# A hybrid decoder layer on one core: 64 more tokens take their first expert product from gathered rows, and the blocks are staged anew

## The chip, the core and the metric

The kernel runs on one core of one Trainium2 chip. A core has five engines that run their own instruction queues in order: TensorE (PE, with its weight loads shown apart as PEld), VectorE (DVE), ScalarE (ACT), GpSimd (POOL) and SyncE (SP), which here only issues DMAs. The metric is the device time of one execution in microseconds (us); lower is better.

## The reference, cut to what matters

One layer on 512 tokens of width 1024: normalisation, three kinds of attention, an output projection, and then a feed-forward part (PEER) that picks experts. All that changes lies in PEER:

```
qry = (h @ w_q) ...                       # 8 heads
s1, s2 = qry halves @ sub1, sub2          # 128 scores each
top 16 of each, top 16 of their sums  ->  expert (8 x 16 = 128 slots per token), gate = softmax
a   = einsum('cd,ced->ce', x, u[expert])  # first product: 16384 experts, rows of 1024
w   = gelu(a) * gate
out = einsum('ce,ced->cd', w, v[expert])  # second product
```

## The kernel before, in words

Tokens are cut into four chunks of 128. **Chunk 0** is done as the reference says: for each of its 128 slots an indirect DMA on POOL gathers one row of `u` per token (`gather`, four row buffers), and one DVE instruction multiplies it with the token's vector and sums it up (line 481, "dot" below). After a gelu the same is done with rows of `v` (line 488).

**Chunks 1 to 3** (384 tokens) are done densely: the 16384 experts are 128 blocks of 128. For a block `a_block` computes the product of the block of `u` with all 384 tokens, in split precision: both sides are cut into a high and a low part (`split`, lines 85 and 86: ACT makes the high part, DVE the low one), and `mm3` does three matmuls for each of eight slices of the width, so 24 matmuls of 384 columns. ACT takes the gelu out of PSUM, where two banks ("t") hold such products. `w_block` multiplies it with the gates of this block (`gt`, zero where a token did not pick the expert), splits the product and the block of `v`, and adds 18 matmuls of 512 columns to the output.

The gates come from a table `gd` in DRAM (12 pieces of 32 tokens). It is written in the **scatter stage**: for each four tokens DVE makes one-hot rows (line 586, then four times line 590), PE multiplies them (line 593) and ACT copies the result (line 594). There are 96 such groups of four. No `w_block` can run before all of the table is written.

So blocks of `u` come in two kinds. **Early blocks** (`NSP`, 64) only need `a_block`, and run beside routing and scatter; their gelus go to DRAM (`ad`) and come back later, but for the last `KEEP` = 16, which stay in SBUF ("kept"). The room of the kept tiles is that of the scatter stage's tiles, so the kept blocks run after it. The other blocks run together with the `w_block`s of all 128 in the **last stage**. After each early block one step of chunk 0's gathers follows in the program text.

The order on each engine is not that of the program text: it is set when the kernel is built, by a scheduler which estimates when each instruction can start. Each engine then runs its list in order.

Of the kernel before, what the change touches and what calls it, by code (L numbers as in the profile page):

```python
# [22 lines left out]
P = 128  # L23
# [14 lines left out]
NSP = 64  # L38
# [9 lines left out]
KEEP = 16  # L48
TD = P * len(DC)
# [6 lines left out]
def layer_kernel(ctx, tc, x, xT, memT, mem, w_in, w_kv, w_out, w_q, cols, qk_gain, g_bc, subT, bias_tab,  # L56
# [11 lines left out]
    gd = dram.tile([TD // GT, P, NK, GT], F32, name="gd")  # L68
# [285 lines left out]
    def mix_out(chunks, yT, rg, hT, name):  # L354
        n_c = len(chunks)
        with tile_pool(name=f"wo{name}", bufs=2) as wo:
# [55 lines left out]
    def route(c, dst=None, q0=0, nq=PH):  # L412
# [95 lines left out]

    def u_parts(b, i, e_lo):
        ur = flat().rearrange("p (k e) -> p k e", e=NK)  # L510
        DMA.dma_start(ur, uT[b])
        halves[b] = [t.rearrange("p k t -> p (k t)")[:, i * D:(i + 1) * D].rearrange("p (k e) -> p k e", e=NK)
                     for t in yT]
        last_lo.append(split(*halves[b], ur, e_lo))

    def a_block(b):
        us = halves.pop(b)
        ap = bank("t")[:, :TD]
        for k in range(KD):
            mm3(ap, [t[:, k, :] for t in us], [t[:, k, S - TD:] for t in hT], k == 0, k == KD - 1)  # L520
# [7 lines left out]
    with tile_pool(name="qa", bufs=1) as qa, tile_pool(name="qp", bufs=2) as qp:  # L528
        mix_out([GC] + DC, yT, rg, hT, "l")
        G.memset(ga[0], 0.0)  # L530
        rp = ctx.enter_context(tile_pool(name="rp", bufs=1, side="right"))
        sub = qa.tile([P, 2 * PH, NK], F32, name="sub", bufs=1)
        for n in range(4):
# [25 lines left out]
            for i in range(4):  # L559
                m = 4 * n + i  # L560
                acc = bank("s")[:, :TD]
                for k in range(KD):
                    mm3(acc, [t[:, i, k % 2, :] for t in w[k // 2]], [t[:, k, S - TD:] for t in hT],
                        k == 0, k == KD - 1)
                qy = qp.tile([P, TD], F32, tag="qy", name="qy")
                A.activation(qy, acc, AF.Copy)
                sc = quarters(bank("o"))[:, 0:len(DC), :]
                for j in range(len(DC)):
# [4 lines left out]
                      [ti[c][m % 2][:, m // 2, :] for c in DC], qp, "r")  # L573
    loaded = 0
    steps = gather_all()
    with tile_pool(name="oh", bufs=2) as oh:
        for ci_, c in enumerate(DC):
            iT = oh.tile([P, 3, P], F32, tag="iT", name="iT")
            route(c, iT)
            for q in range(P // GT):  # L580
                stage = oh.tile([P, NK, GT], F32, tag="stage", name="stage")
                for t4 in range(0, GT, 4):
                    t0 = q * GT + t4
                    o1 = oh.tile([P, 4, NK], F32, tag="o1", name="o1", bufs=3)
                    o2 = oh.tile([P, 4, NK], F32, tag="o2", name="o2", bufs=3)
                    V.tensor_tensor(o1, iT[:, 0, t0:t0 + 4, None].to_broadcast([P, 4, NK]),  # L586
                                    iota[:, None, :].to_broadcast([P, 4, NK]), ALU.is_equal)
                    for j in range(4):
                        i2, gate = (iT[:, i, t0 + j:t0 + j + 1] for i in (1, 2))
                        V.tensor_scalar(o2[:, j, :], iota, i2, gate, ALU.is_equal, ALU.mult)  # L590
                    gp = quarters(bank("s"))
                    for j in range(4):
                        T.matmul(gp[:, j, :], o1[:, j, :], o2[:, j, :], start=True, stop=True)  # L593
                    A.activation(stage[:, :, t4:t4 + 4].rearrange("p e t -> p t e"), gp, AF.Copy)  # L594
                DMA.dma_start(gd[ci_ * (P // GT) + q], stage)
# [13 lines left out]
    with tile_pool(name="vb", bufs=2) as vb:  # L609
# [14 lines left out]
        def w_block(n, b, ag):  # L624
# [6 lines left out]
            if g0 not in gtiles:  # L631
                gt = vb.tile([P, TD // GT, NB, GT], F32, tag="gt", name="gt")
# [102 lines left out]
```

## Time and profile before

| | us |
|---|---|
| median of 3 runs | 1700.32 (1698.85 to 1704.48) |
| the profiled execution, its own time | 1705.15 |
| span in its trace | 1703.4 |
| PE busy | 1596.3 (94%) |
| DVE busy | 1304.5 (77%) |
| ACT busy | 675.2 (40%) |
| POOL busy | 467.0 (27%) |

The shares are means over stages with different limits: up to about 310 us projection and attention, then output projection, query and routing, from about 570 to 817 us the scatter stage, and from there the last stage. An engine that is never idle in a stretch sets its length. In the view by windows an engine that is busy for the whole window shows the window's length. A matmul's duration overlaps the next one's, so PE's rate is read from the distance of starts. A matmul of plain fp32 operands shows as two records.

### The profile page before, as it was taken

To read this page: it belongs to the slowest core of one execution; us is meant where nothing else is said; L and a number is where in the kernel's file an instruction comes from. 1 tells how busy PE (TensorE), PEld (TensorE's weight loads), DVE (VectorE), ACT (ScalarE), POOL (GpSimd) and SP (SyncE) were. 2 spreads that over 40 slices of the span, in tenths; PEclk is the share of its full clock that TensorE was granted. 3 is DMA by queue.
4 is the path that set the end of the run, shared out by engine and by line. 5 is a ranking of instruction groups with operands and counts; after the bars stand their busy time and mean duration, and the time that the engine had idled before them with its cause. 6 is when DMAs were issued, how large, how long until landed. Compare 5 with 4: busy or idle time off the path is not lost.

```text
span 1703.4 us, 22918 instructions
## 1 busy us (share of the span) xinstructions
PE 1596.3 (94%) x8045; PEld 1405.0 (82%) x8045; DVE 1304.5 (77%) x2983; ACT 675.2 (40%) x1031; POOL 467.0 (27%) x338
## 2 busy tenths in 40 slices
PE   8999989998999995767799999999999999999998
PEld 6887667998999995656798988888888888888887
DVE  5656756699999999999468888778788878744444
ACT  6344544233434454456333333333333333333332
POOL 4320013252324242110145434334433343200000
PEclk9999999999999997689999999999999999999999
DMA  8312034133888785324689999999999999844533
GB/s 315 99 50 106 1 116 156 50 112 104 269 280 290 241 304 193 124 105 186 260 263 347 343 354 327 317 344 342 339 339 322 320 355 346 265 150 151 164 124 136
DMA packets 159763, 383.73 MB, mean 225 GB/s; under 512 B 12192, under 2 KB 82848, under 8 KB 156960
## 3 DMA queue, kind: packets, MB, share of 16 engines
q1 hardware_dynamic: 122784, 248.04, 41.9%
q0 software_dynamic: 36864, 134.23, 22.1%
q8 instruction: 63, 1.03, 0.2%
q14 instruction: 52, 0.43, 0.1%
HBM read 343.43 MB, written 38.80 MB: 224 GB/s over the span
## 4 chain that ended last, share of the span: by engine, by line
PE 72%; DVE 15%; issue 9%; ACT 1%; DMA 1%; POOL 1%; SPq 0%; DVEq 0%; POOLq 0%; ACTq 0%
PE s L94 9%; PE s L95 9%; PE s L96 9%; PE t L96 9%; PE t L94 9%; PE t L95 9%; PE o L95 4%; PE o L94 4%; PE o L96 4%; DVE o L590 2%; PE o L329 2%; DVE yT L86 2%; PE s L297 1%; DVE row L481 1%; DVE o L586 1%
## 5 line engine op out<-in xcount | busy, mean ns | idle before, releaser
L94 PE MATMUL t<-hT,yT 128*128 128x384 f32 x1024 | 346.6, 339 | 8.2 <-ACT kept L525 6.8
L96 PE MATMUL t<-hT,yT 128*128 128x384 f32 x1024 | 346.7, 339 | 6.3 <-DVE yT L86 6.3
L95 PE MATMUL t<-hT,yT 128*128 128x384 f32 x1024 | 345.8, 338 | 0.0
L474 POOL DMA_INDIRECT row<-u,exp_g x128 | 163.6, 1278 | 422.5 <-DVE row L481 316.4
L85 ACT ACTIVATE yT<-flat 128x1024 fp32r<-128x1024 f32 x128 | 135.7, 1060 | 275.6 <-PE t L95 167.1
L474 POOL DMA_INDIRECT row<-v,exp_g x128 | 163.0, 1273 | 258.1 <-DVE ga L488 235.7
L86 DVE TENSOR_TENSOR yT<-flat,yT 128x1024 fp32r<-128x1024 f32 x128 | 163.5, 1277 | 81.4 <-ACT yT L85 77.0
L86 DVE TENSOR_TENSOR yT<-vr,yT 128x1024 fp32r<-128x1024 f32 x128 | 156.4, 1222 | 72.2 <-ACT yT L85 72.0
L94 PEld LDWEIGHTS t<-hT,yT 128*128 128x128 f32 x1024 | 194.1, 190 | 14.7 <-ACT kept L525 7.3
L95 PE MATMUL s<-yT,ws 128*128 128x512 f32 x512 | 202.8, 396 | 0.0
L96 PEld LDWEIGHTS t<-hT,yT 128*128 128x128 f32 x1024 | 194.0, 189 | 10.1 <-DVE yT L86 6.9
L95 PEld LDWEIGHTS t<-hT,yT 128*128 128x128 f32 x1024 | 194.1, 190 | 4.5
L85 ACT ACTIVATE ws<-w 128x384 fp32r<-128x384 f32 x128 | 67.1, 525 | 314.6 <-issue 125.6
L96 PE MATMUL s<-yT,ws 128*128 128x512 f32 x512 | 191.4, 396 | 0.0
L593 PE MATMUL s<-o,o 128*128 128x128 f32 x768 | 127.6, 321 | 56.9 <-DVE o L590 55.7
L85 ACT ACTIVATE yT<-vr 128x1024 fp32r<-128x1024 f32 x128 | 134.5, 1051 | 100.8 <-PE o L96 77.9
L593 PEld LDWEIGHTS s<-o,o 128*128 128x128 f32 x768 | 114.6, 223 | 69.7 <-issue 55.8
L94 PE MATMUL s<-yT,ws 128*128 128x512 f32 x512 | 170.5, 396 | 0.0
L481 DVE SCALAR_TENSOR_TENSOR row<-row,hg 128x1024 f32<-128x1024 f32 x128 | 159.2, 1252 | 9.0 <-DMA row<-u,exp_g 9.0
L488 DVE SCALAR_TENSOR_TENSOR ga<-row,gw,ga 128x1024 f32<-128x1024 f32 x128 | 163.7, 1279 | 2.8 <-DMA row<-v,exp_g 2.0
L86 DVE TENSOR_TENSOR ws<-w,ws 128x384 fp32r<-128x384 f32 x128 | 70.6, 555 | 86.0 <-ACT ws L85 83.8
L594 ACT ACTIVATE stage<-s 128x512 f32<-128x512 f32 x96 | 101.3, 1073 | 83.8 <-PE s L593 83.8
(266 smaller groups left out, 2825.9 us busy)
## 6 DMA issues: line engine op xcount, KB each, us to landing
flat<-uT SPq DMA_DIRECT2D x128, 512.0 KB, 5.1
vr<-v SPq DMA_DIRECT2D x128, 512.0 KB, 5.4
gd<-stage SPq DMA_DIRECT2D x12, 2048.0 KB, 6.3
gt<-gd SPq DMA_DIRECT2D x32, 768.0 KB, 8.2
ad<-ag SPq DMA_DIRECT2D x48, 192.0 KB, 5.0
agr<-ad SPq DMA_DIRECT2D x48, 192.0 KB, 8.8
wraw<-w_in SPq DMA_DIRECT2D x8, 1024.0 KB, 5.1
flat<-w_q SPq DMA_DIRECT2D x16, 512.0 KB, 3.9
```

The lines of the kernel that those rows point to most:

```text
L85: A.activation(hi, src, AF.Copy)
L86: return (e_lo or V).tensor_sub(lo, src, hi.bitcast(F32))
L94: T.matmul(o, ah, bh, start=start, stop=False)
L95: T.matmul(o, ah, bl, start=False, stop=False)
L96: T.matmul(o, al, bh, start=False, stop=stop)
L329: T.matmul(o_ps[:, q0:W], l, r, start=n_ == 0, stop=n_ == len(mms) - 1)
L474: G.indirect_dma_start(out=row, out_offset=None, in_=table, in_offset=bass.IndirectOffsetOnAxis(ap=exp_g[:, s_:s_ + 1], axis=0))
L481: V.scalar_tensor_tensor(row, row, 1.0, hg, ALU.mult, ALU.mult, accum_out=av[:, s_:s_ + 1])
L488: V.scalar_tensor_tensor(ga[0], row, gw[:, s_:s_ + 1], ga[0], ALU.mult, ALU.add)
L590: V.tensor_scalar(o2[:, j, :], iota, i2, gate, ALU.is_equal, ALU.mult)
L593: T.matmul(gp[:, j, :], o1[:, j, :], o2[:, j, :], start=True, stop=True)
L594: A.activation(stage[:, :, t4:t4 + 4].rearrange("p e t -> p t e"), gp, AF.Copy)
```

## The change

Chunk 1's first 64 tokens leave the dense first product.

- Their `u` rows are gathered: 64 gathers of 128 rows, with slots 0 to 63 of the 64 tokens on the lower half of the partitions and slots 64 to 127 on the upper one (`exp_x`; `hx` holds the tokens' vectors twice). The 64 dots (`dot`, line 494) are written into the scatter loop, one per group of four tokens.
- Their gelu is multiplied into the gates before those are scattered, so their two pieces of `gd` come last; in `w_block` an ACT copy (line 697) brings the two pieces in, and the DVE product covers the other 320 tokens.
- `a_block` has 320 columns in place of 384.
- `NSP` is 80 and `KEEP` 8: 72 early blocks go through DRAM, 8 are kept.
- The 16 odd early blocks from 49 on (`whole`) are not split: 8 plain fp32 matmuls with `hF`, the sum of the tokens' two parts, which POOL makes once.

```diff
-NSP = 64
+NSP = 80
-KEEP = 16
-TD = P * len(DC)
+KEEP = 8
+WHOLE = 48
+HX = P // 2
+DX = DC[0]
+T0 = DX * P + HX
+TQ = P * len(DC)
+TD = S - T0
...
+        if extra:
+            ids, gates, cols_ = extra
+            A.activation(cols_[:, 0:2, :], tp[:, 0:2, 0:HX], AF.Copy)
+            A.activation(gates, gt, AF.Copy)
+            A.activation(ids[0:HX, :], ei[0:HX, 0:HX], AF.Copy)
+            DMA.dma_start(ids[HX:P, :], ei[0:HX, HX:P])
...
+    def dot(s_, h, to, ids=exp_g):
+        row = gather(u, s_, ids)
+        V.scalar_tensor_tensor(row, row, 1.0, h, ALU.mult, ALU.mult, accum_out=to[:, s_:s_ + 1])
...
+    def whole(b):
+        return WHOLE <= b < NSP and b % 2 == 1
...
+        if whole(b):
+            halves[b] = [ur]
+            return
...
-            mm3(ap, [t[:, k, :] for t in us], [t[:, k, S - TD:] for t in hT], k == 0, k == KD - 1)
+            if whole(b):
+                T.matmul(ap, us[0][:, k, :], hF[:, k, :], start=k == 0, stop=k == KD - 1)
+            else:
+                mm3(ap, [t[:, k, :] for t in us], [t[:, k, T0:] for t in hT], k == 0, k == KD - 1)
...
+    G.tensor_add(hF, hT[0][:, :, T0:].bitcast(F32), hT[1][:, :, T0:].bitcast(F32))
...
+                A.activation(stage[:, :, t4:t4 + 4].rearrange("p e t -> p t e"), gp, AF.Copy)
+                s_ = next(early, None) if dots else None
+                if s_ is not None:
+                    dot(s_, hx, avx, exp_x)
...
+        A.activation(ax[0:HX, 0:HX], avx[0:HX, :], AF.Copy)
+        DMA.dma_start(ax[0:HX, HX:P], avx[HX:P, :])
+        A.activation(ax[0:HX, :], ax[0:HX, :], AF.Gelu)
+        V.tensor_mul(gx[0:HX, :], gx[0:HX, :], ax[0:HX, :])
+        tp = quarters(bank("o"))
+        T.transpose(tp[:, 0, :], gx, ident)
+        A.activation(iX[:, 2, :], tp[:, 0, 0:HX], AF.Copy)
+        for q in range(HX // GT):
+            scatter(DX, iX, q, q * GT, False)
...
-            V.tensor_mul(by_q(w), by_q(ag), gt[:, :, b % NB, :])
+            A.activation(by_q(w[:, 0:HX]), gt[:, 0:HX // GT, b % NB, :], AF.Copy)
+            V.tensor_mul(by_q(w[:, HX:]), by_q(ag), gt[:, HX // GT:, b % NB, :])
```

What the scheduler makes of it is seen in the engines' lists. **First place, DVE**, early in the scatter stage. `o` is a one-hot tile, `yT<-flat` the low part of a block of `u`, `row,av<-row,hg` a dot of chunk 0 and `row,avx<-row,hx` one of the 64 tokens. Before:

```order
L586 TENSOR_TENSOR o_4618<-iT,iota 128x512
L590 TENSOR_SCALAR o_4619<-iota,iT 128x128 x4
L441 TENSOR_TENSOR eq<-eq,ci 128x800 x2
L446 TENSOR_TENSOR pe<-wv,wm 128x128
L86 TENSOR_TENSOR yT_1426<-flat,yT_1425 128x1024
L481 SCALAR_TENSOR_TENSOR row,av<-row,hg 128x1024
L86 TENSOR_TENSOR yT_1426<-flat,yT_1425 128x1024
L481 SCALAR_TENSOR_TENSOR row,av<-row,hg 128x1024
L86 TENSOR_TENSOR yT_1426<-flat,yT_1425 128x1024
L481 SCALAR_TENSOR_TENSOR row,av<-row,hg 128x1024
L586 TENSOR_TENSOR o_4631<-iT,iota 128x512
```

The same place after the change:

```order
L92 TENSOR_TENSOR yT_1451<-flat,yT_1450 128x1024 x2
L621 TENSOR_TENSOR o_4683<-iT,iota 128x512
L625 TENSOR_SCALAR o_4684<-iota,iT 128x128 x4
L621 TENSOR_TENSOR o_4699<-iT,iota 128x512
L625 TENSOR_SCALAR o_4700<-iota,iT 128x128 x4
L621 TENSOR_TENSOR o_4715<-iT,iota 128x512
L625 TENSOR_SCALAR o_4716<-iota,iT 128x128 x4
L494 SCALAR_TENSOR_TENSOR row,avx<-row,hx 128x1024 x4
L450 TENSOR_REDUCE ex<-eq 128x16 x2
L457 TENSOR_REDUCE sg<-pe 128x8
```

Chunk 0's dots have moved behind the 64 new ones, which stand in fours. Counted along DVE's list up to the last one-hot row, there were 54 splits of blocks of `u` and 51 dots before; now there are 63 splits and 105 dots (64 and 41).

**Second place, PE**, late in the scatter stage. `t<-hT,yT` is a matmul of a split block, `t<-hF,flat` one of a whole block, `s<-o,o` one of the scatter. Before, only scatter matmuls stood here:

```order
L593 MATMUL s<-o_5439,o_5438 128x128 x4
L593 MATMUL s<-o_5452,o_5451 128x128 x4
L593 MATMUL s<-o_5467,o_5466 128x128 x4
L593 MATMUL s<-o_5480,o_5479 128x128 x4
L593 MATMUL s<-o_5493,o_5492 128x128 x4
```

And now:

```order
L628 MATMUL s<-o_5890,o_5889 128x128 x2
L102 MATMUL t<-hT_2658,yT_1451 128x320
L544 MATMUL t<-hF,flat 128x320 x2
L628 MATMUL s<-o_5906,o_5905 128x128 x4
L544 MATMUL t<-hF,flat 128x320 x5
L628 MATMUL s<-o_5922,o_5921 128x128 x4
L544 MATMUL t<-hF,flat 128x320
L628 MATMUL s<-o_5940,o_5939 128x128 x4
```

The blocks reach much further into the scatter stage. Counted along PE's list, 1872 of 3072 block matmuls stood behind the last scatter matmul before; now 1224 split ones and 24 whole ones stand there. The 2304 matmuls of the `w_block`s all stand behind it, before and now. The last 32 groups of the scatter still have nothing between them.

**Third place, ACT**, from the end of the scatter stage. `kept<-t` is the gelu of a kept block, which frees its bank "t"; `w<-gt` the new copy of gates. Before:

```order
L594 ACTIVATE stage<-s 128x4x128 x42
L525 ACTIVATE kept_7852<-t 128x384
L525 ACTIVATE kept_7886<-t 128x384
L85 ACTIVATE yT_1425<-flat 128x1024
L525 ACTIVATE kept_7920<-t 128x384
L85 ACTIVATE yT_1425<-flat 128x1024
L525 ACTIVATE kept_7954<-t 128x384
```

And now:

```order
L629 ACTIVATE stage<-s 128x4x128 x30
L551 ACTIVATE kept_8714<-t 128x320
L551 ACTIVATE kept_8732<-t 128x320
L91 ACTIVATE yT_1450<-flat 128x1024
L551 ACTIVATE kept_8764<-t 128x320
L697 ACTIVATE w<-gt 128x64 x2
L551 ACTIVATE kept_8782<-t 128x320
```

Two copies of gates now stand ahead of the fourth kept gelu.

## Rows read from the trace of the kernel before

**Rows 1.** The page: engines' busy tenths and granted clock, 40 slices of 42.6 us.

```profile
PE   8999989998999995767799999999999999999998
DVE  5656756699999999999468888778788878744444
PEclk9999999999999997689999999999999999999999
```

**Rows 2.** Windows: stretch, us, then PE, PEld, DVE, ACT, POOL busy, clock, DMA.

```profile
400.00:640.00 240.00, 232.93 (x1358) 230.99 (x1359) 240.00 (x744) 101.25 (x135) 81.16 (x58) 0.98 0.77 259
640.00:817.00 177.00, 118.53 (x697) 105.21 (x696) 175.56 (x469) 91.54 (x89) 20.22 (x10) 0.84 0.36 145
920.00:1690.00 770.00, 770.00 (x3656) 668.57 (x3655) 549.69 (x654) 270.21 (x367) 220.34 (x171) 1.00 0.81 283
```

**Rows 3.** Timeline of DVE's last scatter operation: start, us, what.

```profile
814.47 1.10 DVE L590 TENSOR_SCALAR o<-iota,iT 128x128 f32<-128x128 f32 x4
```

**Rows 4.** Timeline of PE: first block matmul behind the scatter, last matmul.

```profile
817.54 0.44 PE L94 MATMUL t<-hT,yT 128*128 128x384 f32 x1 [1.43 <-ACT kept L525]
...
1696.91 0.40 PE L96 MATMUL o<-yT,ws 128*128 128x512 f32 x1
```

**Rows 5.** Timeline of PE: block matmuls 47 apart, and output matmuls 11 apart.

```profile
609.81 0.33 PE L95 MATMUL t<-hT,yT 128*128 128x384 f32 x1
...
617.95 0.34 PE L94 MATMUL t<-hT,yT 128*128 128x384 f32 x1
...
1690.12 0.39 PE L95 MATMUL s<-yT,ws 128*128 128x512 f32 x1
...
1692.70 0.40 PE L96 MATMUL o<-yT,ws 128*128 128x512 f32 x1
```

**Rows 6.** Timeline of DVE: split, dot, split; two scatter groups; the same beside POOL.

```profile
606.64 1.22 DVE L86 TENSOR_TENSOR yT<-flat,yT 128x1024 fp32r<-128x1024 f32 x1
607.78 1.22 DVE L481 SCALAR_TENSOR_TENSOR row<-row,hg 128x1024 f32<-128x1024 f32 x1
...
608.92 1.22 DVE L86 TENSOR_TENSOR yT<-flat,yT 128x1024 fp32r<-128x1024 f32 x1
...
611.21 0.69 DVE L586 TENSOR_TENSOR o<-iT,iota 128x512 f32<-128x512 f32 x1
...
612.84 0.68 DVE L586 TENSOR_TENSOR o<-iT,iota 128x512 f32<-128x512 f32 x1
...
618.01 2.66 DVE L86 TENSOR_TENSOR yT<-flat,yT 128x1024 fp32r<-128x1024 f32 x1
620.59 2.78 DVE L481 SCALAR_TENSOR_TENSOR row<-row,hg 128x1024 f32<-128x1024 f32 x1
```

**Rows 7.** Timeline of POOL in that stretch.

```profile
617.23 5.06 POOL L441 TENSOR_TENSOR eq<-eq,ci 128x800 f32<-128x800 f32 x2 [4.52 <-DVE eq L439]
```

**Rows 8.** Groups by form: line, operation, tiles, shapes, count, busy, mean ns, idle.

```profile
L86 POOL TENSOR_TENSOR lo<-flat,hi 128x1024 fp32r<-128x1024 f32 x18 | 43.0, 2412 | 48.8 <-ACT hi L85 48.8
...
L329 PE MATMUL o<-pT,vt 128*128 128x512 f32 x24 | 12.4, 597 | 0.1
...
L329 PE MATMUL o<-pT,vt 128*128 128x128 f32 x24 | 4.6, 274 | 0.0
```

**Rows 9.** The page, DMA issues: KB each, median us to landing.

```profile
gd<-stage SPq DMA_DIRECT2D x12, 2048.0 KB, 6.3
gt<-gd SPq DMA_DIRECT2D x32, 768.0 KB, 8.2
```

**Rows 10.** DMA from 900 to 1450 us: all packets; gathers and their landing.

```profile
DMA packets 84273, 185.74 MB, mean 338 GB/s; under 512 B 5920, under 2 KB 45344, under 8 KB 84237
...
row<-v,exp_g POOLq DMA_INDIRECT x122, 7.1
row<-u,exp_g POOLq DMA_INDIRECT x52, 7.2
```

**Rows 11.** All gathers, landing.

```profile
DMA to landing us min/median/max: 4.4/6.8/11.4
```

More of the change, by code (lines that the diff above doesn't have):

```diff
@@ L397, in mix_out @@
                     split(hi, lo, quarters(t_ps))
+                if c == DX:
+                    DMA.dma_start(hd, h[0:HX, :])
     def top16(n, src, vals, idx, pool, tag):
@@ L470, in route, with gather @@
         A.activation(dst, tp, AF.Copy)
-    def gather(table, s_):
+        if extra:
[4 more added lines that the diff above has]
+            DMA.dma_start(ids[HX:P, :], ei[0:HX, HX:P])
+    def gather(table, s_, ids=exp_g):
         row = gr.tile([P, D], F32, tag="row", name="row")
         G.indirect_dma_start(out=row, out_offset=None, in_=table,
-                             in_offset=bass.IndirectOffsetOnAxis(ap=exp_g[:, s_:s_ + 1], axis=0))
+                             in_offset=bass.IndirectOffsetOnAxis(ap=ids[:, s_:s_ + 1], axis=0))
         return row
+    def dot(s_, h, to, ids=exp_g):
+        row = gather(u, s_, ids)
+        V.scalar_tensor_tensor(row, row, 1.0, h, ALU.mult, ALU.mult, accum_out=to[:, s_:s_ + 1])
     def gather_all():
         for s_ in range(NSLOT):
-            row = gather(u, s_)
-            V.scalar_tensor_tensor(row, row, 1.0, hg, ALU.mult, ALU.mult, accum_out=av[:, s_:s_ + 1])
+            dot(s_, hg, av)
             yield
@@ L531, in layer_kernel @@
         rp = ctx.enter_context(tile_pool(name="rp", bufs=1, side="right"))
+        hx = rp.tile([P, D], F32, name="hx")
+        for i in range(2):
+            DMA.dma_start(hx[i * HX:(i + 1) * HX, :], hd)
+        exp_x = rp.tile([P, HX], I32, name="exp_x")
+        avx = rp.tile([P, HX], F32, name="avx")
+        gx, ax = (rp.tile([P, NSLOT], F32, name=n_) for n_ in ("gx", "ax"))
         sub = qa.tile([P, 2 * PH, NK], F32, name="sub", bufs=1)
@@ L560, in layer_kernel @@
                 m = 4 * n + i
-                acc = bank("s")[:, :TD]
+                acc = bank("s")[:, :TQ]
                 for k in range(KD):
-                    mm3(acc, [t[:, i, k % 2, :] for t in w[k // 2]], [t[:, k, S - TD:] for t in hT],
+                    mm3(acc, [t[:, i, k % 2, :] for t in w[k // 2]], [t[:, k, S - TQ:] for t in hT],
                         k == 0, k == KD - 1)
-                qy = qp.tile([P, TD], F32, tag="qy", name="qy")
+                qy = qp.tile([P, TQ], F32, tag="qy", name="qy")
                 A.activation(qy, acc, AF.Copy)
@@ L573, in layer_kernel @@
                       [ti[c][m % 2][:, m // 2, :] for c in DC], qp, "r")
+    wp = ctx.enter_context(tile_pool(name="wp", bufs=1))
+    hF = wp.tile([P, KD, TD], F32, name="hF")
+    G.tensor_add(hF, hT[0][:, :, T0:].bitcast(F32), hT[1][:, :, T0:].bitcast(F32))
     loaded = 0
@@ L576, in layer_kernel @@
     with tile_pool(name="oh", bufs=2) as oh:
-        for ci_, c in enumerate(DC):
-            iT = oh.tile([P, 3, P], F32, tag="iT", name="iT")
[L579 to L595, printed above, removed]
@@ new lines, in layer_kernel, with scatter @@
+        iX = oh.tile([P, 3, HX], F32, name="iX", bufs=1)
+        early = iter(range(HX))
+        def scatter(c, iT, q, col, dots):
+            stage = oh.tile([P, NK, GT], F32, tag="stage", name="stage")
+            for t4 in range(0, GT, 4):
+                t0 = col + t4
+                o1 = oh.tile([P, 4, NK], F32, tag="o1", name="o1", bufs=3)
+                o2 = oh.tile([P, 4, NK], F32, tag="o2", name="o2", bufs=3)
+                V.tensor_tensor(o1, iT[:, 0, t0:t0 + 4, None].to_broadcast([P, 4, NK]),
+                                iota[:, None, :].to_broadcast([P, 4, NK]), ALU.is_equal)
+                for j in range(4):
+                    i2, gate = (iT[:, i, t0 + j:t0 + j + 1] for i in (1, 2))
+                    V.tensor_scalar(o2[:, j, :], iota, i2, gate, ALU.is_equal, ALU.mult)
+                gp = quarters(bank("s"))
+                for j in range(4):
+                    T.matmul(gp[:, j, :], o1[:, j, :], o2[:, j, :], start=True, stop=True)
+                A.activation(stage[:, :, t4:t4 + 4].rearrange("p e t -> p t e"), gp, AF.Copy)
+                s_ = next(early, None) if dots else None
+                if s_ is not None:
+                    dot(s_, hx, avx, exp_x)
+            DMA.dma_start(gd[(c - DX) * (P // GT) + q], stage)
@@ new lines, in layer_kernel @@
+        for c in DC:
+            iT = oh.tile([P, 3, P], F32, tag="iT", name="iT")
+            route(c, iT, extra=(exp_x, gx, iX) if c == DX else None)
+            for q in range(HX // GT if c == DX else 0, P // GT):
+                scatter(c, iT, q, q * GT, True)
+        for s_ in early:
+            dot(s_, hx, avx, exp_x)
+        A.activation(ax[0:HX, 0:HX], avx[0:HX, :], AF.Copy)
+        DMA.dma_start(ax[0:HX, HX:P], avx[HX:P, :])
+        A.activation(ax[0:HX, :], ax[0:HX, :], AF.Gelu)
```

11 lines of the change are left out of this document (6 added, 5 removed).

## The prediction

> **What bounds the kernel now.** I read the page's slices first [rows 1], then the windows [rows 2], then timelines at the stages' edges. The slices show two regimes: PE at 9 nearly everywhere, but with a dent from slice 16 to 20 (640 to 850 us), where DVE stands at 9. The windows make it exact. From 400 to 640 us DVE is busy for all 240 us, and from 640 to 817 us for 175.6 of 177, while PE has 118.5. From 920 to 1690 us PE is busy for all 770 us and DVE for 550 [rows 2]. So up to 817 us DVE sets the pace, and behind it PE. The edge is the end of the scatter stage: DVE's last one-hot row ends at 814.47 + 1.10 = 815.6 us [rows 3], PE's first block matmul behind it starts at 817.5 and its last matmul ends at 1697.3 us [rows 4].
>
> Is PE really full there? Block matmuls stand (617.95 - 609.81)/47 = 0.1732 us apart, output matmuls (1692.70 - 1690.12)/11 = 0.2345 us [rows 5]. Behind the scatter stand 1872 and 2304 of them: 324.2 + 540.3 = 864.5 us of the 879.8 us. So 15.3 us are lost there, and 6.1 us follow up to 1703.4. The profile adds up as 815.6 (DVE) + 1.9 + 864.5 (PE) + 15.3 + 6.1.
>
> The change moves work from the PE term to the DVE term. I price both.
>
> **The DVE term.** Up to the last one-hot row DVE has 9 more splits and 54 more dots. Split to dot and dot to split are 1.14 us apart [rows 6]; 63 x 1.14 = 71.8 us. The number of groups (96, 1.63 us each [rows 6]), routing and query work stay. All of it counts, since DVE has no idle time there that could take it. The early blocks that are whole cost DVE nothing here, which is why 75 blocks are ready with 63 splits.
>
> Three smaller costs.
> - hF is one POOL addition of 2560 elements: 2.41 us for 1024 [rows 8] gives 6.0 us. When POOL multiplied for 5.06 us [rows 7], a split and a dot of DVE took 618.01 to about 623.3, 5.3 us in place of 2.28 [rows 6]: 3.0 us lost, 0.6 per us of POOL. So 3.6 us; I take 4, bounds 0 and 6. On this the Trainium skill ("SBUF — State Buffer", section "SBUF: two separate sides") says that a VectorE operation with two SBUF inputs and a GpSimd operation that reads SBUF lock each other out for a whole instruction. By that rule hF would cost its 6.0 us, two more than I take; the row says that DVE gets something done in between.
> - The first of the 64 dots needs `exp_x`: a cast, an ACT copy, a small DMA, then a gather that lands in about 7 us [rows 10]. DVE's list has some 11 us of other work between the cast and that dot. The trace has no such chain: 0 if it fits, 8 if the small DMA takes as long as a gather; I take 3.
> - The other dots can wait for their rows. A row buffer is free again when its dot ends, so the gather four dots later has the DVE work in between to land. Adding DVE's distances along the list, before this was never under 12.1 us; now it is 8.3 at the least and 12.2 in the median. A gather lands 7.2 us after its issue even at full DMA load [rows 10], plus about 1 us until POOL issues it: 8 us, just under the least. I take 4 us. The floor is 0. The ceiling: each landing takes the longest, 11.4 [rows 11]; then each four dots come 12.0 - 8.3 = 3.7 us late, 26 times, 96 us.
>
> DVE's last one-hot row then ends at 815.6 + 71.8 + 4 + 3 + 4 = 898.4 us.
>
> PE must be done with 61 split and 13 whole blocks by then. That is 1464 x 0.146 + 104 x 0.54 (below) = 270 us, with some 65 us of scatter and queries, in about 390 us before the last 32 groups. It fits, with less margin than the count says if its clock falls.
>
> **The PE term.** A block matmul has 320 columns in place of 384. The two distances give (0.2345 - 0.1732)/128 = 0.48 ns per column, so 0.1425 us; keeping a fixed part of 13 ns at 2.4 GHz gives 0.1466. I take 0.146. The upper end is 0.1732, if the distance is not set by columns. Then 1224 x 0.146 = 178.7 us. A whole block has 8 fp32 matmuls of two records: (597 - 274)/384 = 0.84 ns per column and record [rows 8], 0.27 us for 320, 0.54 for a matmul; 24 x 0.54 = 13.0 us. (Over 16 blocks this is 69 us where split ones would take 56, for 16 x 1.14 us of DVE: PE pays where it has room.) The outputs stay at 540.3. Sum 732.0, which is 132.5 less.
>
> What DVE and DMA have to do beside it must keep up. Through the middle of the last stage one gather came per 3.33 us of PE work (162 over 88 `w_block`s and 40 blocks), and PE was never idle [rows 2]. Now it is one per 3.53 us (182 over 120 and 39), so the pace is no tighter; but it no longer stops 200 us ahead of the end.
>
> **The start of the last stage** is where I expect PE to lose most. ACT's two copies of gates wait for `gt`, which waits for the last piece of `gd`: 6.3 + 8.2 us [rows 9] plus the last copy, some 17 us behind the last group. The fourth kept gelu stands behind them, so its bank is held, and PE, which needs that bank again two blocks on, waits for it about 5 us (17 us less what PE still has of early blocks). DVE's list has 9 dots and then 4 more before the first `w` is made, at the gathers' pace, so that the first output matmul starts some 8 us after PE has run out. With the usual losses later I take 20 us in place of 15.3; 8 if all is there in time, 40 if both waits repeat.
>
> Sum: 898.4 + 1.9 + 732.0 + 20 + 6.1 = 1658.4 us of span. The profiled execution takes 1705.15 for a span of 1703.4, so 1.75 is added: 1660.2. It lies 4.8 above the median of its runs, so I forecast 1660.2 - 4.8 = **1655 us**.
>
> Other edits: more traffic through `ad` (72 x 160 KB each way for 48 x 192), 16 kept tiles fewer, an ACT copy of 64 elements per block. ACT was busy for 270 of 770 us and DMA for 81% [rows 2]: hidden, and if they are not, they show in the 20 us.
>
> **Rivals.**
> - *Rows come late (slower).* The place is DVE's list in the scatter stage, where fours of dots stand 8.3 us apart. Each us of landing above 7.7 costs up to 26 us. The forecast turns into a loss from 1700 - 1655 = 45 us, so from a landing of about 9.5 us; at 10 us it is 60 less the 4 counted: 1711. For it: the new gathers share the DMAs with blocks, `ad` and 2 MB pieces of `gd`. Against it: at 338 GB/s half of the landings were within 7.2 us [rows 10], and DMA had 36 to 77% here [rows 2]. The last stage could do the same: 396 transfers of 0.524 MB, 25 of `gt`, 12 of `agr` make 245 MB, 724 us at 338 GB/s, hardly less than PE's 732. The Trainium skill ("DMA: Bandwidth & Descriptors", "Where 436 GB/s comes from") puts HBM's limit for a core at about 358 GB/s; by that figure it would be an estimated 683 us. No run here shows 358. Chance 7%.
> - *Columns don't count.* Were a block matmul to stay at 0.1732, the PE term would be 1224 x 0.027 = 33 us more: 1688, half of the gain. Against it: 128 columns more cost 61 ns between the two distances. 6%.
> - *PE becomes late in the scatter stage.* With gaps between its blocks its granted clock falls: 0.84 from 640 to 817 us [rows 2], where it had too little to do. At the lower level a block takes twice as long and DVE waits for it. A PE that is late is also full, and from 400 to 640 us a full PE had 0.98. I price it at 20 us: 1675. 12%.
> - *Nothing waits.* No late row, no hF, a clean start: 11 + 9 us less, 1635. 15%.
>
> **Chances.** The forecast's own case has 60% (1645 to 1668). The range 1634 to 1692 leaves out most of the first rival and little else. About 0.3%, 5 us, is what a measurement of this kernel can tell from no change. Faster by more than that: 60 + 15 + 12 and half of the second rival, 90%; within it 5%, slower 5%.
>
> **What would show it.** DVE's last one-hot row at 885 to 905 us, with DVE busy throughout; PE's block matmuls 0.146 us apart and fp32 records of 320 columns 0.27; PE from there to its last matmul 740 to 760 us, idle 10 to 25 of them in the first 60. I am wrong if DVE shows waits for `row<-u` of tens of us in the scatter stage, if that row comes after 930 us, or if PE waits on loads throughout the last stage.

## The result, and the profile after

The changed kernel takes 1652.64 us (median of 4 runs, 1650.69 to 1653.16) where the kernel before took 1701.85 us beside it (1698.85 to 1704.48): a ratio of 0.9709, 95% interval 0.9689 to 0.9729. The forecast was 1655 us. The profiled execution took 1650.69 us for a span of 1648.9.

The page's slices (41.2 us each here) answer to [rows 1]: the dent of PE now lies from 824 to 948 us (the digits 6, 6 and 7), and DVE is full ahead of it.

```profile
PE   8999989898999878899866799999999999999998
DVE  6666755599999999999998588787888788787886
PEclk9999999998999999999956999999999999999999
```

The windows (columns as in [rows 2]) say how full the engines were:

```profile
400.00:640.00 240.00, 208.21 (x1327) 202.75 (x1328) 235.87 (x736) 98.45 (x138) 87.43 (x47) 0.93 0.63 220
640.00:817.00 177.00, 161.23 (x969) 141.23 (x968) 172.92 (x383) 75.01 (x93) 75.03 (x52) 0.97 0.86 309
817.00:900.00 83.00, 53.23 (x235) 48.04 (x236) 81.64 (x205) 33.06 (x33) 35.05 (x29) 0.60 0.81 291
900.00:1640.00 740.00, 730.88 (x3560) 621.98 (x3560) 582.92 (x733) 281.58 (x488) 259.22 (x210) 0.99 0.93 331
```

DVE is the full engine up to 900 us (490 of 500 us busy) and PE behind it, as before. PE, which was full from 400 to 640 us before (233 of 240 us), now waits there as well (208). DMA has risen to 0.93 of its share in the last stage, from 0.81.

The edges, in the timelines of DVE and PE (start, us, what), answer to [rows 3, 4]:

```profile
895.34 1.11 DVE L625 TENSOR_SCALAR o<-iota,iX 128x128 f32<-128x128 f32 x4
```

```profile
899.29 0.63 PE L100 MATMUL t<-hT,yT 128*128 128x320 f32 x1 [1.41 <-ACT kept L551]
899.72 0.47 PE L101 MATMUL t<-hT,yT 128*128 128x320 f32 x1
899.99 0.47 PE L102 MATMUL t<-hT,yT 128*128 128x320 f32 x1
...
916.82 4.57 PE L544 MATMUL t<-hF,flat 128*128 128x320 f32 x16 [3.41 <-ACT kept L551]
920.99 0.55 PE L100 MATMUL t<-hT,yT 128*128 128x320 f32 x1
...
930.89 6.88 PE L544 MATMUL t<-hF,flat 128*128 128x320 f32 x16 [4.10 <-DMA flat<-uT]
937.36 0.55 PE L100 MATMUL t<-hT,yT 128*128 128x320 f32 x1
937.90 0.31 PE L102 MATMUL t<-hT,yT 128*128 128x320 f32 x1
...
944.50 0.31 PE L102 MATMUL t<-hT,yT 128*128 128x320 f32 x1
944.64 0.39 PE L100 MATMUL s<-yT,ws 128*128 128x512 f32 x1
...
1643.40 0.40 PE L102 MATMUL o<-yT,ws 128*128 128x512 f32 x1
```

DVE's last one-hot row ends at 895.34 + 1.11 = 896.45 us; PE works from 899.29 to 1643.80 and 5.1 us follow. So the span is 896.45 + 2.84 + 744.5 + 5.1: the DVE term grew by 80.9 us against before, and PE's shrank by 135.3. A block matmul of 320 columns takes (944.50 - 937.90)/45 = 0.1467 us. At the edge the same matmuls stood 0.267 us apart (899.72 to 899.99): the granted clock was 0.60 from 817 to 900 us, where PE had only one-hot products to do up to 899 us, and PE began the last stage at the lower of its two levels (0.51 from 899 to 905 us).

What DVE and PE waited for (views by waits: engine, line, releaser: us in total, times, longest), DVE from 314.4 to 896.5 us and PE from 897 to 1642 us:

```profile
DVE tv L410 <- ACT sx L587: 15.9, 1, 15.9
DVE row L494 <- DMA row<-u,exp_x: 2.5, 3, 1.2
DVE o L621 <- PE s L628: 2.2, 1, 2.2
DVE row L494 <- DMA row<-u,exp_g: 1.9, 2, 1.2
DVE ex L450 <- POOL eq L449: 1.7, 1, 1.7
DVE yT L92 <- ACT yT L91: 1.1, 1, 1.1
```

```profile
PE t L544 <- DMA flat<-uT: 4.1, 1, 4.1
PE t L544 <- ACT kept L551: 3.4, 1, 3.4
PE t L102 <- DVE yT L92: 1.6, 1, 1.6
PE t L100 <- ACT kept L551: 1.4, 1, 1.4
```

The first wait of DVE, 15.9 us, ends as its work of this stretch begins, at 314.47 us; the others make 9.4 us, of which late rows are 4.4.

### The profile page after: what moved, and what is told of

It is laid out like the page before. It is cut to its first block, busy times and chain, and to the rows that moved or that the text cites. A ratio compares the mean times of both kernels' runs of the same rounds, so it can differ in the third digit from the quotient of the medians.

```text
span 1648.9 us, 23114 instructions
## 1 busy us (share of the span) xinstructions
PE 1528.8 (93%) x7918; PEld 1318.3 (80%) x7918; DVE 1348.3 (82%) x3096; ACT 669.9 (41%) x1149; POOL 560.0 (34%) x403
## 4 chain that ended last, share of the span: by engine, by line
PE 62%; DVE 27%; DMA 5%; issue 3%; ACT 2%; POOL 1%; ACTq 0%; DVEq 0%; SPq 0%; POOLq 0%
PE s L100 9%; PE s L101 9%; PE s L102 9%; PE t L100 5%; DVE row L494 5%; PE t L101 5%; PE t L102 5%; PE o L100 4%; PE o L101 4%; PE o L102 4%; DVE o L625 4%; DVE yT L92 3%; DVE o L621 3%; PE o L335 2%; DMA flat<-uT 2%
## 5 line engine op out<-in xcount | busy, mean ns | idle before, releaser
L102 PE MATMUL t<-hT,yT 128*128 128x320 f32 x896 | 285.5, 320 | 31.0 <-DVE yT L92 30.9
L100 PE MATMUL t<-hT,yT 128*128 128x320 f32 x896 | 288.7, 322 | 14.4 <-ACT ag L551 12.4
L101 PE MATMUL t<-hT,yT 128*128 128x320 f32 x896 | 284.4, 317 | 0.0
L488 POOL DMA_INDIRECT row<-v,exp_g x128 | 155.0, 1211 | 288.6 <-DVE ga L505 268.0
L102 PEld LDWEIGHTS t<-hT,yT 128*128 128x128 f32 x896 | 174.2, 195 | 38.4 <-DVE yT L92 34.0
L101 PE MATMUL s<-yT,ws 128*128 128x512 f32 x512 | 202.2, 396 | 0.0
L102 PE MATMUL s<-yT,ws 128*128 128x512 f32 x512 | 196.3, 396 | 0.0
L100 PEld LDWEIGHTS t<-hT,yT 128*128 128x128 f32 x896 | 174.6, 195 | 23.8 <-ACT ag L551 16.0
L91 ACT ACTIVATE yT<-flat 128x1024 fp32r<-128x1024 f32 x112 | 118.5, 1058 | 171.2 <-DMA flat<-uT 85.8
L101 PEld LDWEIGHTS t<-hT,yT 128*128 128x128 f32 x896 | 174.6, 195 | 5.1
L494 DVE SCALAR_TENSOR_TENSOR row<-row,hg 128x1024 f32<-128x1024 f32 x128 | 154.3, 1220 | 21.1 <-DMA row<-u,exp_g 21.0
L92 DVE TENSOR_TENSOR yT<-flat,yT 128x1024 fp32r<-128x1024 f32 x112 | 147.1, 1322 | 19.7 <-ACT yT L91 16.3
L628 PE MATMUL s<-o,o 128*128 128x128 f32 x768 | 124.0, 316 | 31.3 <-DVE o L625 31.3
L100 PE MATMUL s<-yT,ws 128*128 128x512 f32 x512 | 151.9, 394 | 0.0
```

The source lines that it names most:

```text
L91: A.activation(hi, src, AF.Copy)
L92: return (e_lo or V).tensor_sub(lo, src, hi.bitcast(F32))
L100: T.matmul(o, ah, bh, start=start, stop=False)
L101: T.matmul(o, ah, bl, start=False, stop=False)
L102: T.matmul(o, al, bh, start=False, stop=stop)
L488: G.indirect_dma_start(out=row, out_offset=None, in_=table, in_offset=bass.IndirectOffsetOnAxis(ap=ids[:, s_:s_ + 1], axis=0))
```

## The experiments

Ratios are to runs of the kernel before on the same chip, with 95% intervals; the changed kernel has 0.9709 (0.9689 to 0.9729). Where the edge of two profiled executions is compared, one thing has to be taken off: DVE's first instruction of routing, ahead of every edit, starts at 314.5 us in the changed kernel's profile, but at 317.6 in e1's, 316.8 in e3's, 319.25 in e4's and 317.65 in e6's.

### No unsplit blocks (e1)

```diff
-WHOLE = 48
+WHOLE = NSP
...
-    hF = wp.tile(...)
-    G.tensor_add(hF, ...)
+    hF = None
```

> The changed kernel with no unsplit blocks: all 80 early blocks are split, and hF is not made. Theory (DVE sets the end of the scatter stage, PE has room there): up to the last one-hot row DVE has 15 more splits and 5 more dots in its list, 20 x 1.14 = 22.8 us, less about 4.5 us that hF held a split; PE has 1296 split matmuls behind it, 190 us, in place of 1224 and 24 whole ones, 192 us. So the last one-hot row ends near 915 us and the time is about 16 us longer: 1669 us. Rival (PE is late in the scatter stage): the 16 whole blocks cost PE 0.75 us more each than split ones, 12 us, so the time falls to about 1643 us.

Measured: 1666.40 us, 0.9791 (0.9769 to 0.9814), 0.8% above the changed kernel. DVE's last one-hot row ends at 919.35 us, 22.9 later, and PE's stretch from its first block matmul (922.18 us) to its last is 7.6 us shorter.

```profile
918.22 1.13 DVE L623 TENSOR_SCALAR o<-iota,iX 128x128 f32<-128x128 f32 x4
```

Of the 22.9 us, 3.1 stand ahead of routing, so 19.8 are left for the edit, for 22.8 - 4.5 = 18.3 counted. Of the 7.6 us, 2 were counted; PE's waits behind the edge are 6.5 us in place of 10.5, and no unsplit block stands there. The theory holds: where DVE sets the edge, a split costs its full length, and PE, which is busy for 406 of the 500 us from 400 to 900 us here and for 423 in the changed kernel, pays for the whole blocks out of waits.

### Only the gathered tokens (e2)

```diff
-NSP = 80
+NSP = 64
-KEEP = 8
+KEEP = 16
-WHOLE = 48
+WHOLE = NSP
...
-    G.tensor_add(hF, ...)
+    hF = None
```

> Only the gathered tokens: the changed kernel with 64 early blocks, 16 of them kept, as before, and none unsplit. Theory: against the kernel before, DVE has 58 more dots ahead of its last one-hot row, 66 us, and a few us of late rows; PE has the same 1872 block matmuls behind it, 0.0265 us shorter each, 50 us. So it is slower than before, by some 15 to 22 us: about 1720 us. The rival (the gathered tokens bring the gain, since 64 columns fewer in 128 blocks are 81 us of PE): about 1640 to 1660 us.

Measured: 1722.97 us, 1.0125 (1.0103 to 1.0146): slower than the kernel before, at the forecast place. In the profiles DVE's last one-hot row ends 71.6 us later than before, and PE's stretch behind it is 57.6 us shorter. PE finds nothing to do with the freed time. In the windows it was busy for 103 of 177 us from 640 to 817 us, at a clock of 0.66 (the window, and DVE's last one-hot row):

```profile
640.00:817.00 177.00, 103.23 (x513) 94.52 (x512) 173.31 (x393) 63.23 (x66) 82.84 (x58) 0.66 0.72 251
```

```profile
886.05 1.13 DVE L623 TENSOR_SCALAR o<-iota,iX 128x128 f32<-128x128 f32 x4
```

### Only the new staging (e3)

The kernel before, with 384 columns and no gathered tokens:

```diff
-NSP = 64
+NSP = 80
-KEEP = 16
+KEEP = 8
+WHOLE = 48
...
+            if whole(b):
+                T.matmul(ap, us[0][:, k, :], hF[:, k, :], ...)
...
+    hF = wp.tile([P, KD, TD], F32, name="hF")
+    G.tensor_add(hF, ...)
```

> Only the staging: the kernel before with 80 early blocks, 8 kept, 16 unsplit, and no gathered tokens (384 columns, hF with 3072 elements). By the two lists: DVE has 9 more splits and 24 more dots of chunk 0 ahead of its last one-hot row, 37.6 us, and hF, 5 us; PE has 1224 split and 24 whole matmuls behind it, 212 + 15.5 us in place of 324: 97 us less. If DVE sets the pace that is 54 us less, about 1648 us, no worse than the whole change. The rival: with 384 columns PE has 74 blocks, about 320 us, to do in the scatter stage beside queries and one-hot products, is late there, and the time is 1665 to 1685 us.

Measured: 1654.87 us, 0.9722 (0.9698 to 0.9746). The interval overlaps that of the whole change: **nearly all of the gain comes from the staging, and the gathered tokens on top of it bring nothing that these runs can tell**. In the windows PE is full where it waits in the changed kernel; the line after them is DVE's last one-hot row:

```profile
400.00:640.00 240.00, 224.90 (x1296) 221.73 (x1297) 240.00 (x734) 94.46 (x128) 86.75 (x57) 0.97 0.73 242
640.00:817.00 177.00, 174.32 (x982) 145.50 (x981) 172.24 (x395) 82.95 (x97) 61.77 (x34) 1.00 0.78 277
```

```profile
865.40 1.25 DVE L603 TENSOR_SCALAR o<-iota,iT 128x128 f32<-128x128 f32 x4
```

The last one-hot row ends at 866.65 us, 8.6 later than counted (2.6 of them ahead of routing), and PE's stretch behind it is 779.8 us. Against the changed kernel the one is 29.8 us earlier and the other 35.3 longer. The lists say where the 29.8 come from: here 75 dots of chunk 0 stand ahead of the edge, with the gathered tokens 41. So the 64 new dots push 34 old ones behind it and cost only 30 x 1.14 = 34 us there, about what 64 columns give PE back. In e2 they pushed only 6 back: by the count they cost 66 us and PE gave back 50. The rival was right that PE is full here, but wrong in its price. Of the staging's three parts only the unsplit blocks were taken out alone (e1); more early blocks and fewer kept ones were not tried apart.

### hF added up three times (e4)

```diff
     G.tensor_add(hF, hT[0]..., hT[1]...)
+    G.tensor_add(hF, hT[0]..., hT[1]...)
+    G.tensor_add(hF, hT[0]..., hT[1]...)
```

> The changed kernel with hF added up three times, one after the other, on POOL. If each addition holds DVE's two-input operations for its whole length (a split took 5.67 us beside the one addition), two more cost 2 x 4.5 to 2 x 5.8 us, 9 to 12 us; by the prediction's price of 0.6 us per us of POOL they cost 7 us; if it holds nothing, 0.

Measured once: 1665.45 us, and the last one-hot row ends 15.2 us later than in the changed kernel, 4.8 of them ahead of routing. The 10.4 that are left lie within the first price and above the second, but one edge can't tell the two apart: in e6 it moved by 5.8 us, behind the start of routing, that no edit is known to have caused. What was held decides. The additions on POOL, and what DVE ran meanwhile (rows above 1.1 us long):

```profile
445.18 5.73 POOL L608 TENSOR_TENSOR hF<-hT,hT 128x2560 f32<-128x2560 f32 x1
450.99 6.55 POOL L609 TENSOR_TENSOR hF<-hT,hT 128x2560 f32<-128x2560 f32 x1
457.62 6.67 POOL L610 TENSOR_TENSOR hF<-hT,hT 128x2560 f32<-128x2560 f32 x1
```

```profile
446.35 5.65 DVE L92 TENSOR_TENSOR yT<-flat,yT 128x1024 fp32r<-128x1024 f32 x1
453.66 3.96 DVE L436 TENSOR_TENSOR cv<-tv,tv 128x64 f32<-128x64 f32 x1
457.55 1.21 DVE L92 TENSOR_TENSOR yT<-flat,yT 128x1024 fp32r<-128x1024 f32 x1
459.22 5.11 DVE L464 CAST exp_g<-ex 128x32 int32<-128x32 f32 x1
```

Each addition holds one DVE instruction until it ends: the split is done at 452.0 us, one split's length after the first addition's end at 450.9; the small addition `cv` at 457.6, the second's end; the cast at 464.3, the third's. Between two additions DVE gets one instruction in (the split at 457.55). The two extra ones held `cv` for about 3.8 us and the cast for about 5.0, 8.8 together; DVE's busy time up to the edge is 8.6 us above that of the changed kernel (581.2 against 572.6).

### The copy of gates on DVE (e5)

```diff
-            A.activation(by_q(w[:, 0:HX]), gt[...], AF.Copy)
+            V.tensor_copy(by_q(w[:, 0:HX]), gt[...])
```

> The changed kernel with the copy of gates into w on DVE in place of ACT, so that no gelu stands behind a wait for gt. Theory of the last stage's start: PE's wait of 3.4 us for a kept gelu behind the two copies goes, and DVE has room for 128 copies of some 0.2 us (it is busy for 583 us of 740): 2 to 4 us faster, about 1649 us. Rival: what comes next there, the load of the next block (PE waited 4.1 us for flat), is late whatever ACT does, and the time stays at 1652 us; or the copies on DVE delay the splits, and it is a few us slower.

Measured: 1652.35 us, 0.9696 (0.9678 to 0.9714): no change that can be told. The gelu behind the copies is earlier (909.16 in place of 916.35 us), but then ACT waits for `vr`. ACT's timeline, first of the changed kernel, then of e5:

```profile
916.04 0.40 ACT L697 ACTIVATE w<-gt 128x64 f32<-128x64 f32 x2 [9.18 <-DMA gt<-gd]
916.35 0.42 ACT L551 ACTIVATE kept<-t 128x320 f32<-128x320 f32 x1
```

```profile
909.16 0.44 ACT L551 ACTIVATE kept<-t 128x320 f32<-128x320 f32 x1 [3.12 <-issue]
918.20 1.06 ACT L91 ACTIVATE yT<-vr 128x1024 fp32r<-128x1024 f32 x1 [8.59 <-DMA vr<-v]
```

PE still waits 8.9 us behind the edge (4.2 for kept gelus, 2.4 for a split, 2.3 for a load) in place of 10.5: the loads are late, whatever ACT does.

### More for PE to do ahead of the last stage (e6)

```diff
-                for j in range(4):
+                for j in [j_ for _ in range(1 if dots else 2) for j_ in range(4)]:
                     T.matmul(gp[:, j, :], o1[:, j, :], o2[:, j, :], ...)
```

> The changed kernel with each matmul of the last 16 one-hot groups made twice (the result is the same), so that PE has more to do ahead of the last stage. PE's first 21 matmuls there stood 0.267 us apart in place of 0.147, 2.4 us lost, and one unsplit block took 2.3 us longer. If PE's own work ahead sets the granted clock, it starts at the upper level: 2 to 5 us faster, 1648 us. If the doubled matmuls make PE late for the groups (four matmuls took 2.05 us at the lower level, a group comes each 2.7 us on average): 10 to 20 us slower. If neither, no change.

Measured: 1658.64 us, 0.972 (0.9697 to 0.9744), not to be told apart from the changed kernel. The clock did what was expected: over the doubled groups (858 to 905 us) the granted clock is 0.88 where the changed kernel has 0.62 (852 to 896 us), and the first block matmuls come at the upper level's distance at once:

```profile
908.57 0.31 PE L101 MATMUL t<-hT,yT 128*128 128x320 f32 x1
908.72 0.31 PE L102 MATMUL t<-hT,yT 128*128 128x320 f32 x1
```

But PE's stretch is 742.9 us in place of 744.5: 1.6 us, a little below the 2 to 5; its waits for late gelus and loads behind the edge are 10.5 us as before. The last one-hot row also came 9.0 us later: 3.2 of them ahead of routing, 2 more by the first one-hot row, where new rows are later (3.7 us of waits for 1.8), all ahead of the edited groups, and the rest with late rows of chunk 0 (5.8 us of waits for 1.9). That these are the edit's doing is not shown.

### 88 and 96 early blocks (e7, e8)

```diff
-NSP = 80
-WHOLE = 48
+NSP = 88          # e8: 96
+WHOLE = 40        # e8: 32
```

> The changed kernel with 88 early blocks, the 24 odd ones from 41 on unsplit. DVE's list up to its last one-hot row has 5 dots fewer, 5.7 us; PE has 1032 split and 24 whole matmuls behind it in place of 1224 and 24, 28 us less. If PE has room in the scatter stage for 8 more whole blocks (34 us; it waited some 80 us there): 34 us faster than the changed kernel, 1619 us. Rival (PE or the loads are late there: DMA is at 0.81 to 0.86 from 640 to 900 us): 1635 to 1650 us.

Measured for e7: 1627.27 us, 0.9549 (0.9523 to 0.9575), 1.6% under the changed kernel. PE has the room: from 640 to 900 us it is busy for 233 of 260 us in place of 214. Its last matmul ends at 1613.10 us, 30.7 earlier than in the changed kernel, yet the span is only 22.3 us shorter. PE no longer ends last: chunk 0's last row of `v` is added 5.2 us after it, which neither forecast had. PE's last matmul, then DVE's last additions of rows:

```profile
1612.71 0.40 PE L102 MATMUL o<-yT,ws 128*128 128x512 f32 x1
```

```profile
1615.72 2.60 DVE L505 SCALAR_TENSOR_TENSOR ga<-row,gw,ga 128x1024 f32<-128x1024 f32 x2
```

> The changed kernel with 96 early blocks, the 32 odd ones from 33 on unsplit. DVE's list has 1 split and 9 dots fewer, 11.4 us; PE has 840 split and 24 whole matmuls behind it, 56 us less. If PE has room for 16 more whole blocks, 68 us: 68 us faster than the changed kernel, 1585 us. Rival (PE, with some 80 us of waits there, and the loads become the bound of the scatter stage): the gain stops at about 35 us, 1615 to 1635 us.

Measured for e8: 1631.48 us, 0.9563 (0.9538 to 0.9587): the gain stops, as the rival said, but not for its reason (e8's time can't be told from e7's). The last one-hot row ends at 893.99 us, and PE's last matmul at 1599.6 us, 13.5 earlier than in e7. What ends last, by 30 us now, is chunk 0's second product on DVE:

```profile
1599.16 0.40 PE L102 MATMUL o<-yT,ws 128*128 128x512 f32 x1
```

```profile
1624.63 5.25 DVE L505 SCALAR_TENSOR_TENSOR ga<-row,gw,ga 128x1024 f32<-128x1024 f32 x4 [3.64 <-DMA row<-v,exp_g]
```

The rows of `v` come 3.2 us apart (128 from 1224 to 1630 us). In the changed kernel the last of them was added at 1622 us, 22 us ahead of PE's end: that was all the margin, and e7 had already used it up.

### The new dots at half their width (e9)

```diff
         row = gather(u, s_, ids)
-        V.scalar_tensor_tensor(row, row, 1.0, h, ...)
+        n = D if h is hg else D // 2
+        V.scalar_tensor_tensor(row[:, 0:n], row[:, 0:n], 1.0, h[:, 0:n], ...)
```

> The changed kernel with each of the 64 new dots taken over 512 of the 1024 elements only (half of that sum is left out), which frees the row buffers earlier. DVE's list up to the last one-hot row is then 64 x 0.53 us shorter, and 21 dots of chunk 0 fewer stand in it: 58 us. If DVE alone set the end of the scatter stage, that row ends near 838 us and the time falls to 1595 us. If rows come late (the first rival of the prediction), DVE shows waits for rows of 20 us or more there and much of this is lost. If what ends last then is chunk 0's gathers, 21 more of them in the last stage at 3.3 to 3.4 us each, 236 rows from 840 us on end near 1630 us: 1635 us.

Measured: 1625.18 us, 0.9569 (0.9523 to 0.9615), 10 us under the 1635 expected. All three parts are seen (the last one-hot row; the last three rows of `v`, after a wait):

```profile
838.91 1.10 DVE L626 TENSOR_SCALAR o<-iota,iX 128x128 f32<-128x128 f32 x4
```

```profile
1610.27 3.93 DVE L506 SCALAR_TENSOR_TENSOR ga<-row,gw,ga 128x1024 f32<-128x1024 f32 x3 [2.62 <-DMA row<-v,exp_g]
```

The last one-hot row ends at 840.0 us, 56.4 earlier for 58 counted; DVE's waits for the new rows grow from 2.5 to 9.2 us, which is the first rival's mechanism, real but small, even with the row buffers freed earlier; and PE is done at 1586.6 us while chunk 0's rows end at 1614. The path changed hands, so 56 us at the edge were worth 27 by the medians, 24 by the ratios.

### Fewer kept blocks and more row buffers (e10 to e12)

e10 and e11 take e7's 88 early blocks with `KEEP` = 4, e12 with `KEEP` = 0; e11 has a fifth row buffer in the last stage, e12 a fifth and a sixth:

```diff
-KEEP = 8
+KEEP = 4          # e12: 0
...
-        row = gr.tile([P, D], F32, tag="row", name="row")
+        pool = (["gr"] * 4 + xpool)[next(xturn) % (4 + len(xpool))]
+        row = (gr if pool == "gr" else pool).tile([P, D], F32, tag="row", name="row")
...
+    with tile_pool(name="r5", bufs=1) as r5:      # e12: bufs=2
+        xpool += [r5] * 1                       # e12: * 2
```

> The kernel of e7 (88 early blocks) with 4 kept ones in place of 8; the control for the next run. PE has 984 split and 8 whole matmuls behind the last one-hot row in place of 1032 and 24, 16 us less; DVE's list has 3 splits more and 2 dots fewer ahead of it. If PE's remainder sets the end: 1612 us. If chunk 0's gathers end last (in e8 the last row of v was added 30 us after PE's last matmul), no change, 1627 us.

Measured: 1636.62 us, 0.9631 (0.959 to 0.9672). PE's last matmul ends at 1597.3 us, 15.8 earlier than in e7 (16 counted), and the rows of `v` at 1627.7, 9.4 later: slower than e7, since the rows end last. That fits neither value expected (1612 or 1627 us). The rows of `v` begin 20.2 us later than in e7 (1220.1 us); why is not shown.

> The same with a fifth row buffer for chunk 0's gathers in the last stage. If the four buffers times the landing set the pace of the rows (3.3 us each), it falls to 2.7 us, and the rows end 100 us ahead of PE: 1612 us, PE's end. If the DMAs are full there (share 0.95, 340 GB/s in e7), a fifth buffer only makes each row land later: as e10.

Measured: 1621.85 us, 0.9542 (0.9504 to 0.9579); against e10 the intervals are apart; 1612 us was expected if the fifth buffer helped. The rows now end at 1602 us, 26 earlier, but PE only at 1613.5, 16 later: it waited 13.7 us for the high parts of blocks that ACT makes. The two timelines' last rows, DVE then PE:

```profile
1600.76 1.28 DVE L508 SCALAR_TENSOR_TENSOR ga<-row,gw,ga 128x1024 f32<-128x1024 f32 x1
```

```profile
1613.11 0.40 PE L102 MATMUL o<-yT,ws 128*128 128x512 f32 x1
```

DMA moved 344 GB/s from 900 to 1600 us, where e10 moved 338, 2% more. So the fifth buffer did speed up the rows, from 3.2 to 3.0 us apart ((1600.8 - 1219.7)/127), not to 2.7, and something that PE needs came later. That the rows took it from PE's loads fits the DMAs' load, but no wait here shows it.

> The same with no kept blocks and six row buffers in the last stage. PE has 886 split matmuls behind the last one-hot row, 32 us less than in e7; all 88 early blocks go through DRAM. If PE's remainder sets the end: 1600 us. If PE is late with more blocks ahead, or the DMAs are full: 1620 to 1640 us.

Measured: 1639.44 us, 0.9653 (0.9612 to 0.9695). PE waited 22.65 us once behind the edge for a gelu (up to 928.9 us), with no kept block to fill the time until the gates come, and 25.2 us for high parts later; the rows ended at 1566 us, earlier than needed. Of the versions that leave nothing out e11, e7 and e8 are the fastest, 0.9542, 0.9549 and 0.9563, and can't be told apart.

## Why the prediction was right

**The two-term picture held.** Work moved from PE's term to DVE's, and the edge between them moved as counted. Term by term:

| | forecast | measured |
|---|---|---|
| DVE's last one-hot row ends | 898.4 | 896.45 |
| to PE's first block matmul | 1.9 | 2.84 |
| PE's matmuls | 732.0 | 732 |
| lost behind the edge | 20 | 12.5 |
| tail | 6.1 | 5.1 |
| span | 1658.4 | 1648.9 |

PE's matmuls are 1224 x 0.1467 + 48 records x 0.27 + 2304 x 0.234 = 732 us; the measured distance settles the second rival (columns do count: 0.1467, not 0.1732).

**DVE's extra work** was counted as 63 x 1.14 = 71.8 us and 11 of losses. DVE's busy time from 314.4 us to the edge rose from 501.2 to 572.6 us, by 71.4, and its idle time by 9.4. The total is right, its parts are not. The busy time also holds the 4.45 us by which hF held a split (below), so without them it rose by 67 us for 71.8 counted: other work took some 5 us less than before. Chunk 0's dots, for one, took 1.24 us each on the average before, some of them beside POOL, and 1.14 now. The losses are 9.4 + 4.45 = 13.9 us for 11. In them rows cost 4.4 us in place of 4 + 3, but PE, POOL and ACT made DVE wait another 5.0 us that I had not listed. Of these 2.2 us are the third rival's (DVE waiting for PE).

**hF** was given 4 us. The timelines of POOL and DVE show it and a split beside it:

```profile
440.43 5.76 POOL L608 TENSOR_TENSOR hF<-hT,hT 128x2560 f32<-128x2560 f32 x1
```

```profile
441.60 5.67 DVE L92 TENSOR_TENSOR yT<-flat,yT 128x1024 fp32r<-128x1024 f32 x1
447.19 0.67 DVE L416 MAX8 tv<-r 128x8 f32<-128x128 f32 x3
```

The split took 5.59 us to the next start in place of 1.14: 4.45 us lost. The size was right by accident. My price of 0.6 us per us of POOL came from two POOL instructions in a row, between which DVE gets in; beside one, the split was done 1.1 us after the addition's end at 446.19 us, about its usual length. That is the rule of the Trainium skill ("SBUF — State Buffer", "SBUF: two separate sides"), that the loser waits for the whole instruction, and e4 shows it twice more. 1.2 us of the addition cost nothing, because DVE ran a replacement search and a reduction in them, at their usual length.

**The start of the last stage** was the mis-sized term: 20 us forecast, 12.5 measured. Of the two waits that I named, one is there: `gt` came 19.6 us behind the last one-hot row for some 17 counted, and PE waited 3.4 us, for some 5, for the gelu behind the gates' copies. The other is not: the first output matmul follows the last block matmul with no wait (944.50 and 944.64 us). DVE's late dots show elsewhere, as PE's wait of 1.6 us for a split that stood behind this one:

```profile
920.88 1.22 DVE L494 SCALAR_TENSOR_TENSOR row<-row,hg 128x1024 f32<-128x1024 f32 x1 [5.57 <-DMA row<-u,exp_g]
```

The rest I had not named: 4.1 us for a load, and 4.7 us at the lower clock level. PE's first 20 matmuls cost 20 x 0.12 = 2.4 us, and the unsplit block at 930.89 us, after the wait for its load, took 6.47 us to the next start (937.36) in place of the 4.17 of the one at 916.82 (granted clock 0.64 from 930.8 to 937.4 us, 1.00 from 916 to 921). Together that is 13.8 us; the 12.5 are smaller because the 0.234 and 0.27 above are a little more than the outputs and fp32 records took. The forecast had looked for the lower clock further ahead.

**From span to median** I took 3.05 us off, and the profile after stands 3.7 us under its median: before, the profiled execution lay above all of the runs; after, it was the fastest of them. This 6.8 us undid most of the 9.5 by which the span was too long, so 1655 against 1652.64 looks better than the working was: that much of it is luck.

**The first rival** (rows late) was worth 4.4 us. The rows that were late are few: three for the new dots, two for chunk 0. e9 shows that the mechanism exists, with 9.2 us where the dots take half the time. The 358 GB/s that stand beside this rival are no ceiling on short stretches here: from 926 to 937.4 us the DMAs moved 420 GB/s, while the mean over the last stage stayed at 331.

**What the prediction did not separate** is which part pays. It priced tokens and staging together, from one list; e2 and e3 show +1.25% for the first alone and -2.8% for the second alone, and -2.9% for both. The working was right for the list as it stood, but its 71.8 us hide that the staging alone would have pulled 24 dots of chunk 0 ahead of the edge, and that the tokens keep these and ten more behind it.

## What to carry to other kernels

Where a stage is set by one engine and the next by another, price a change as work on either side of the edge between them, by counting what each engine's list really holds ahead of it: the same 64 dots cost 21 us alone and nothing beside a staging in which they push other dots behind the edge. When a change leaves the receiving engine with waits, look for the next cheap unit to move (eight more unsplit blocks here, 25 us), and stop where a third chain comes last, as it already did there; its margin (22 us for chunk 0's rows) can be read beforehand as the distance from its last instruction to the end of the chain that sets the time. A profiled execution is one draw of the spread: a forecast for the median carries its offset, on both sides of the change.

## What the hardware showed

- A POOL addition of 2560 elements held one DVE instruction to its end in three cases: a split (5.67 us in place of 1.22), a small two-input addition (3.96 us in place of 0.20) and a cast with one input (5.11 us). A replacement search (0.27 us) and a reduction (0.97 us) beside it ran at their usual length. Between two such additions in a row DVE got one instruction in.
- After 80 us of one-hot products with gaps PE's clock was at 0.60 to 0.62 and the next stage's first matmuls ran at half speed for 5 us; with the last 16 groups' products made twice it was at 0.88 and they ran at full speed at once. Behind its wait of 4.1 us for a load the unsplit block at 930.89 us ran half of its records at the lower level, 0.53 us apart (6.47 us in all in place of 4.17).
- A block in plain fp32 takes 4.17 us of PE against 24 x 0.1467 = 3.52 us in three fp32r parts, so leaving out the split costs PE 0.65 us and saves DVE 1.14 us.
- 331 to 344 GB/s over 700 us and more, with the DMAs at 0.93 to 0.95, was the most that any version moved over the last stage; in the changed kernel it was 420 GB/s over the 11.4 us from 926 us on.
